# Splitting the weight chunks of two projections: casting and accumulating DMAs in place of a cast and a subtraction

## The chip, the cores and the metric

The kernel runs on one core of a Trainium2 chip. The metric is the device time of one execution in microseconds (us); lower is better.

## What is computed

One layer of an encoder on 512 tokens of width 1024: an input projection, differential attention (8 heads) beside a bidirectional state-space scan (16 heads), an output projection, a layer norm, a gated feed-forward part and a second layer norm. The two projections that the change touches are these, cut from the reference:

```python
mix = jnp.einsum('bse,ed->bsd', jnp.concatenate([attn_out, ssd_out], axis=-1), w_out[l])
x = layernorm(DEEPNORM_ALPHA * x + mix, ln1_g[l], ln1_b[l])
hid = jax.nn.silu(jnp.einsum('bsd,df->bsf', x, w_gate[l])) * jnp.einsum('bsd,df->bsf', x, w_up[l])
ffn = jnp.einsum('bsf,fd->bsd', hid, w_down[l])
x = layernorm(DEEPNORM_ALPHA * x + ffn, ln2_g[l], ln2_b[l])
```

## The kernel before

**Split operands.** TensorE multiplies in `fp32r`, a rounded 32-bit format. To keep float32 accuracy, each operand is split into a high part (rounded) and a low part (the rest), and each product is made of three matmuls: high by high, low by high, high by low (`mm3`, lines 174 to 179; in the out- and down-projections line 177 reads `wh`, line 178 reads `wl`, line 179 `wh` again).

**Weight chunks.** All weights lie in DRAM as `wall`, an array of 130 chunks of 128 x 1024 float32 (512 KB each), in the order in which they are used. Chunks 48 to 63 belong to the output projection (`I_OUT` = 48), 64 to 107 to the feed-forward part, 108 to 129 to the down-projection (`I_DN` = 108). `wload` brings a chunk into a `raw` tile by a DMA on SP's queue (`wr`); `wprep` rounds it to `wh` on ScalarE (line 106) and subtracts to get `wl` on VectorE (line 107). `raw`, `wh` and `wl` are rings of three buffers. `wget` prepares a chunk and the two after it (`AHEAD` = 2), so chunk i+2 is prepared when chunk i is asked for, into the buffers of chunk i-1.

**Out- and down-projection.** `outer_units` runs over chunks: each chunk holds two blocks of 128 rows, each block is multiplied for four tiles of 128 tokens, 24 matmuls of 512 columns for a chunk. The output has two halves of 512 columns, each with its own pass over all rows. The first pass of the output projection (chunks 48 to 55) is woven with the last attention head and goes on behind it. The second passes (`tile_major`) run the first chunks in the same way, and prepare the last four chunks meanwhile into buffers of their own (`hold`: `holdh`, `holdl` in the output projection, `keeph`, `keepl` in the down-projection); these four are then multiplied tile by tile, so that each tile's layer norm can begin early. The down-projection splits its other operand too: `hid_split` rounds a block of `hid` on ScalarE (`hidh`) and subtracts on VectorE (`hidl`).

**Order.** Each engine runs its instructions in order, and waits at the head of its queue. The order on each queue comes from the framework's scheduler, which places the instructions by its own estimate. GpSimd's queue holds few instructions in these stages: a power for each attention head (`f`), two DMAs for each layer norm's scale and shift (`ln`, line 713), and four powers in each layer norm (`rs`, line 729). SP's queue also loads the residual input (`xr` from `in_xs`, line 716) when the attention is done.

Of the kernel before, what the change touches and what calls it, by code (L numbers as in the profile page):

```python
# [8 lines left out]
F32 = mybir.dt.float32  # L9
R32 = mybir.dt.float32r  # L10
AF = mybir.ActivationFunctionType
ALU = mybir.AluOpType
# [16 lines left out]
I_OUT = N_IN  # L29
I_FF = I_OUT + 16  # L30
I_DN = I_FF + 2 * FT
N_W = I_DN + FT
# [18 lines left out]
def encoder(ctx, tc, xt, xs, wall, wdt, consts, masks, vecs, pvec, lnv, out):  # L51
    nc = tc.nc
    V, A, G, T = nc.vector, nc.scalar, nc.gpsimd, nc.tensor
# [38 lines left out]

    wcache = {}
    AHEAD = 2

    def wload(i):
        raw = wp.tile([P, 1024], F32, tag="raw", name=f"wr{i}")
        nc.sync.dma_start(raw, wall[i])
        return raw

    def wprep(i, raw=None, h=None, l=None):
        raw = wload(i) if raw is None else raw
        if h is None:
            h = wp.tile([P, 1024], R32, tag="wh", name=f"wh{i}")
            l = wp.tile([P, 1024], R32, tag="wl", name=f"wl{i}")
        A.copy(h, raw)  # L106
        V.tensor_tensor(l, raw, h.bitcast(F32), op=ALU.subtract)  # L107
        wcache[i] = (h, l)

    def wget(i, ahead=None):  # L110
        for j in range(i, min(N_W, i + 1 + (AHEAD if ahead is None else ahead))):
            if j not in wcache:
                wprep(j)
        return wcache[i]
# [9 lines left out]
    with tc.tile_pool(name="xraw", bufs=1) as xr:  # L124
# [24 lines left out]
        for k in range(KT):  # L149
            A.copy(xh[:, k], raws[k])  # L150
            (G if k in (3, 6) else V).tensor_tensor(xl[:, k], raws[k], xh[:, k].bitcast(F32), op=ALU.subtract)
            if k == 1:
                wprep(0, wraw[0])
        wprep(1, wraw[1])
        for k in range(KT):
            T.matmul(dps[0:32], wdp[:, k], xh[:, k], start=False, stop=False)
# [808 lines left out]
    raw = wload(I_FF + 3)  # L965
# [184 lines left out]
```

## Time and profile before

| what | us |
|---|---|
| median of three runs | 866.48 (865.82 to 866.75) |
| the profiled execution | 866.58 |
| its span, first to last instruction | 864.5 |
| TensorE busy | 848.4 |
| VectorE busy | 615.4 |
| ScalarE busy | 458.4 |
| GpSimd busy | 124.3 |

The profile is that of one execution. A table of busy times tells which engine is full; the waits tell which one holds up the others; and the rows further down are read by stretch, since the stages of this kernel have different limits. Matmuls overlap, so the time of one (some 390 ns) is longer than the distance from one to the next.

### The profile page before, as it was taken

The numbers are of one execution on the slowest core, as the hardware profiler recorded it, in microseconds if no ns is written. First come the engines' busy times: TensorE is split into PE (matmuls) and PEld (weight loads), VectorE is DVE, ScalarE is ACT, GpSimd is POOL, SyncE is SP. The second block draws the span as 40 slices with busy tenths as digits, with TensorE's granted clock in tenths as the row PEclk, the third lists the DMA queues.
The fourth block names the chain that finished last, engine by engine and source line by source line (L and its number), as shares of the span: only waits on it lengthen the run. The fifth ranks groups of instructions, "written<-read, shape, count | busy, mean of one in ns | idle before, by whom it ended". The sixth has DMA issues, their size and how long they took to land.

```text
span 864.5 us, 13803 instructions
## 1 busy us (share of the span) xinstructions
PE 848.4 (98%) x5404; PEld 754.4 (87%) x5404; DVE 615.4 (71%) x1071; ACT 458.4 (53%) x895; POOL 124.3 (14%) x141
## 2 busy tenths in 40 slices
PE   7999999999999999999999999999999999999996
PEld 4798989899889898898888889999999999888885
DVE  4978778775677765777634489898888887734617
ACT  4787666767565655666622215555555565522500
POOL 4016153354500000000000023000000000000002
PEclk9999999999999999999999999999999999999998
DMA  7221211202211202111144501333332333222402
GB/s 261 93 98 49 97 51 50 97 26 74 81 45 71 73 25 88 60 60 62 51 171 146 194 1 41 132 98 104 132 107 98 118 113 137 98 104 91 147 1 97
DMA packets 23008, 78.74 MB, mean 91 GB/s; under 512 B 2688, under 2 KB 2944, under 8 KB 22944
## 3 DMA queue, kind: packets, MB, share of 16 engines
q1 hardware_dynamic: 22320, 75.60, 25.1%
q0 software_dynamic: 624, 2.27, 0.9%
q8 instruction: 42, 0.69, 0.3%
q14 instruction: 22, 0.18, 0.1%
HBM read 75.77 MB, written 2.10 MB: 90 GB/s over the span
## 4 chain that ended last, share of the span: by engine, by line
PE 68%; DVE 2%; ACT 1%; issue 1%; POOLq 0%; POOL 0%; DVEq 0%; ACTq 0%
PE M L892 13%; PE N L892 6%; PE dn L178 4%; PE dn L177 4%; PE dn L179 4%; PE wo L177 3%; PE wo L179 3%; PE wo L178 3%; PE C L892 3%; PE o L623 3%; PE s L596 2%; PE s L597 2%; PE at L611 1%; PE k L177 1%; PE k L179 1%; PE k L178 1%
## 5 line engine op out<-in xcount | busy, mean ns | idle before, releaser
L107 DVE TENSOR_TENSOR wl<-wr,wh 128x1024 fp32r<-128x1024 f32 x101 | 125.3, 1241 | 65.0 <-ACT wh L106 64.9
L106 ACT CAST wh<-wr 128x1024 fp32r<-128x1024 f32 x101 | 105.6, 1048 | 71.0 <-PE wo L179 26.5
L603 ACT ACTIVATE ss<-ss,mn 128x512 f32<-128x512 f32 x64 | 45.9, 718 | 19.7 <-DVE mn L600 19.1
L178 PE MATMUL dn<-wl,hidh 128*128 128x512 f32 x130 | 51.0, 392 | 0.0
L177 PE MATMUL dn<-wh,hidh 128*128 128x512 f32 x130 | 50.9, 392 | 0.0
L179 PE MATMUL dn<-wh,hidl 128*128 128x512 f32 x130 | 50.6, 389 | 0.0
L600 DVE CUSTOM_DVE_ANT_0 ss<-s,tab 128x512 f32<-128x512 f32 x64 | 42.7, 683 | 6.4 <-PE s L597 6.2
L898 ACT COPY e<-M 128x256 f32<-128x256 f32 x60 | 22.3, 372 | 42.1 <-PE M L892 42.0
L458 ACT ACTIVATE rE<-vals,msk 64x128 fp32r<-64x128 f32 x128 | 43.0, 392 | 2.7 <-DVE vals L341 2.1
L177 PE MATMUL wo<-wh,mixh 128*128 128x512 f32 x96 | 38.1, 397 | 0.0
L179 PE MATMUL wo<-wh,mixl 128*128 128x512 f32 x96 | 37.5, 390 | 0.0
L178 PE MATMUL wo<-wl,mixh 128*128 128x512 f32 x96 | 37.4, 390 | 0.0
L177 PE MATMUL z<-wh,xh 128*128 128x256 f32 x128 | 36.4, 286 | 1.0 <-ACT wh L106 1.0
L177 PE MATMUL v<-wh,xh 128*128 128x256 f32 x128 | 36.9, 288 | 0.0
L179 PE MATMUL v<-wh,xl 128*128 128x256 f32 x128 | 36.6, 286 | 0.0
L178 PE MATMUL v<-wl,xh 128*128 128x256 f32 x128 | 36.3, 283 | 0.0
L179 PE MATMUL z<-wh,xl 128*128 128x256 f32 x128 | 36.2, 283 | 0.0
L178 PE MATMUL z<-wl,xh 128*128 128x256 f32 x128 | 36.2, 283 | 0.0
L729 POOL TENSOR_TENSOR rs<-rs,mhalf 128x1 f32<-128x1 f32 x8 | 12.2, 1525 | 158.6 <-DVE rs L728 158.6
L713 POOL DMA_DIRECT2D ln<-in_lnv x4 | 2.3, 578 | 227.1 <-PE dn L178 208.9
L623 PE MATMUL o<-va,as 128*128 128x128 f32 x256 | 34.1, 275 | 0.1
L623 PEld LDWEIGHTS o<-va,as 128*128 128x128 f32 x256 | 31.6, 192 | 0.9 <-ACT osq L626 0.3
(358 smaller groups left out, 2938.2 us busy)
## 6 DMA issues: line engine op xcount, KB each, us to landing
wr<-in_wall SPq DMA_DIRECT2D x130, 512.0 KB, 3.5
xraw<-in_xt SPq DMA_DIRECT2D x8, 256.0 KB, 6.7
xr<-in_xs SPq DMA_DIRECT2D x4, 512.0 KB, 5.2
ln<-in_lnv POOLq DMA_DIRECT2D x4, 512.0 KB, 4.5
out_y<-xr SPq DMA_DIRECT2D x8, 256.0 KB, 2.0
msk<-in_masks SPq DMA_DIRECT2D x1, 490.0 KB, 5.7
cst<-in_consts SPq DMA_DIRECT2D x1, 448.0 KB, 6.7
vec<-in_vecs POOLq DMA_DIRECT2D x1, 168.0 KB, 6.0
```

The source lines that it names most:

```text
L106: A.copy(h, raw)
L107: V.tensor_tensor(l, raw, h.bitcast(F32), op=ALU.subtract)
L177: T.matmul(o, ah, bh, start=first and i == 0, stop=False)
L178: T.matmul(o, ah, bl, start=False, stop=False)
L179: T.matmul(o, al, bh, start=False, stop=last and i == n - 1)
L458: A.activation(r[d][e, h], vals[e, sls[t]], AF.Copy, scale=hmask[e, 4 * g + h:4 * g + h + 1])
L596: T.matmul(sbs[c], QS[:, c, sl], KS[:, c], start=True, stop=False)
L600: V.tensor_tensor_reduce(out=s, in0=sb, in1=tab[:, 384 - 128 * t:896 - 128 * t], scale=1.0, scalar=3.0e38, op0=ALU.add, op1=ALU.min, accum ...
L603: A.activation(s, s, AF.Exp, scale=-1.0, bias=mn[:, t, c:c + 1], accum_out=Z[:, t, c:c + 1])
L623: T.matmul(o, ats[t][:, kt * P:(kt + 1) * P], vv[:, kt, j * P:(j + 1) * P], start=kt == 0, stop=kt == NT - 1)
L892: T.matmul(o, x[:, k], y[:, k], start=first and n == 0, stop=last and n == 11, skip_group_check=True)
L898: mats[j]["i" + name] = A.copy(e, src)
```

## The change

For 34 chunks (50 to 63 and 110 to 129) `wprep` no longer loads a raw tile. The high part is written by a DMA from GpSimd's queue whose destination is `fp32r`, so that the values are rounded on the way. ScalarE then writes the negated high part into the low tile, and a second DMA from GpSimd's queue adds the weights from DRAM to it. The first two chunks of each projection are split as before.

```diff
+    CASTS = [*range(I_OUT + 2, I_FF), *range(I_DN + 2, N_W)]
...
     def wprep(i, raw=None, h=None, l=None):
-        raw = wload(i) if raw is None else raw
+        cast = i in CASTS
+        raw = wload(i) if raw is None and not cast else raw
         if h is None:
             h = wp.tile([P, 1024], R32, tag="wh", name=f"wh{i}")
             l = wp.tile([P, 1024], R32, tag="wl", name=f"wl{i}")
-        A.copy(h, raw)
-        V.tensor_tensor(l, raw, h.bitcast(F32), op=ALU.subtract)
+        if cast:
+
+            nc.gpsimd.dma_start(h, wall[i])
+            A.activation(l, h.bitcast(F32), AF.Copy, scale=-1.0)
+            nc.gpsimd.dma_start(l, wall[i], accum_op=ALU.add)
+        else:
+            A.copy(h, raw)
+            V.tensor_tensor(l, raw, h.bitcast(F32), op=ALU.subtract)
         wcache[i] = (h, l)
```

The change moves instructions on the queues. In the excerpts `wh53`, `wl53` and so on are the high and low tile of chunk 53; the number behind the underscore is a running number of the buffer, and line numbers of the changed kernel from 113 on are 8 higher. GpSimd's queue in the output projection, before, from the powers of heads 6 and 7 to the first layer norm:

```order
L633 TENSOR_TENSOR f6_4374<-f6_4374,mhalf_70 128x4
L633 TENSOR_TENSOR f7_4623<-f7_4623,mhalf_70 128x4
L713 DMA ln0_4812<-in_lnv 128x1024
L713 DMA ln1_4814<-in_lnv 128x1024
L729 TENSOR_TENSOR rs_4755<-rs_4755,mhalf_70 128x1 x4
```

The same queue with the change, from chunk 53 on (line 110 is the casting DMA, line 112 the accumulating one):

```order
L110 DMA wh53_4596<-in_wall 128x1024
L112 DMA wl53_4597<-in_wall 128x1024
L641 TENSOR_TENSOR f7_4619<-f7_4619,mhalf_70 128x4
L110 DMA wh54_4639<-in_wall 128x1024
L112 DMA wl54_4640<-in_wall 128x1024
L110 DMA wh55_4668<-in_wall 128x1024
L112 DMA wl55_4669<-in_wall 128x1024
L110 DMA wh56_4697<-in_wall 128x1024
L110 DMA wh57_4756<-in_wall 128x1024
L112 DMA wl56_4698<-in_wall 128x1024
L721 DMA ln0_4804<-in_lnv 128x1024
L112 DMA wl57_4757<-in_wall 128x1024
```

Up to chunk 55 each chunk's two DMAs stand one behind the other, so the next casting DMA is behind an accumulating one that waits for ScalarE. Behind these rows, with the second pass of the output projection, the four held chunks come in:

```order
L721 DMA ln1_4806<-in_lnv 128x1024
L110 DMA holdh0_4808<-in_wall 128x1024
L110 DMA wh58_4813<-in_wall 128x1024
L110 DMA holdh1_4842<-in_wall 128x1024
L112 DMA holdl0_4809<-in_wall 128x1024
L112 DMA wl58_4814<-in_wall 128x1024
L112 DMA holdl1_4843<-in_wall 128x1024
L110 DMA wh59_4847<-in_wall 128x1024
L110 DMA holdh2_4876<-in_wall 128x1024
L110 DMA holdh3_4905<-in_wall 128x1024
L112 DMA wl59_4848<-in_wall 128x1024
L112 DMA holdl2_4877<-in_wall 128x1024
```

Here the DMAs stand in batches of three of a kind. In the down-projection the queue held, before, the two `ln` loads and the norm's powers:

```order
L820 TENSOR_TENSOR T4_1_5245<-x1h_4757,T2_1_5243 128x512
L820 TENSOR_TENSOR T4_1_5245<-T4_1_5245,x1l_4758 128x512
L713 DMA ln2_8034<-in_lnv 128x1024
L713 DMA ln3_8036<-in_lnv 128x1024
L729 TENSOR_TENSOR rs_4755<-rs_4755,mhalf_70 128x1 x4
```

With the change all four `keeph` and `keepl` pairs and `ln2`, `ln3` stand among the DMAs of chunks 111 to 117, in the first pass. From chunk 119 on a pattern of three chunks repeats:

```order
L112 DMA wl118_8249<-in_wall 128x1024
L110 DMA wh119_8285<-in_wall 128x1024
L110 DMA wh120_8322<-in_wall 128x1024
L112 DMA wl119_8286<-in_wall 128x1024
L112 DMA wl120_8323<-in_wall 128x1024
L110 DMA wh121_8374<-in_wall 128x1024
L112 DMA wl121_8375<-in_wall 128x1024
L110 DMA wh122_8421<-in_wall 128x1024
L110 DMA wh123_8464<-in_wall 128x1024
L112 DMA wl122_8422<-in_wall 128x1024
L112 DMA wl123_8465<-in_wall 128x1024
L110 DMA wh124_8510<-in_wall 128x1024
```

Two chunks go in pairs (wh, wh, wl, wl) and the third alone (wh, wl). On ScalarE's queue a negation stands about where the cast of the chunk stood, on VectorE's queue the subtraction is gone.

## Rows read from the trace of the kernel before

**Rows 1.** The page, busy us, share of the span and instructions of each engine.
```profile
PE 848.4 (98%) x5404; PEld 754.4 (87%) x5404; DVE 615.4 (71%) x1071; ACT 458.4 (53%) x895; POOL 124.3 (14%) x141
```

**Rows 2.** Busy time of each engine by stretch; out-projection, then down-projection.
```profile
core 0: us, PE busy (x) PEld busy (x) DVE busy (x) ACT busy (x) POOL busy (x), PEclk, DMA share, GB/s
...
447.04:463.40 16.36, 16.36 (x74) 13.50 (x73) 3.95 (x4) 3.17 (x3) 0.00 (x0) 1.00 0.52 195
463.40:500.00 36.60, 36.60 (x164) 30.12 (x163) 20.71 (x29) 10.77 (x11) 2.30 (x3) 1.00 0.50 173
739.00:795.00 56.00, 56.00 (x250) 46.03 (x250) 26.90 (x35) 21.57 (x31) 1.12 (x2) 1.00 0.31 109
795.00:840.00 45.00, 45.00 (x239) 38.70 (x238) 19.54 (x27) 13.11 (x16) 0.00 (x0) 1.00 0.22 76
```

**Rows 3.** Waits of TensorE over the whole span, three of eight.
```profile
engine line waited for: us in total, times, longest us
PE dps L148 <- POOL warm L146: 2.5, 1, 2.5
...
PE ff L178 <- DVE x1l L752: 1.1, 1, 1.1
...
PE s L596 <- DVE mixl L389: 0.3, 1, 0.3
```

**Rows 4.** ScalarE in order of time: start, length, instruction, idle before and releaser.
```profile
430.44 1.06 ACT L106 CAST wh<-wr 128x1024 fp32r<-128x1024 f32 x1 [3.16 <-PE wo L179]
...
439.51 1.04 ACT L106 CAST wh<-wr 128x1024 fp32r<-128x1024 f32 x1 [2.38 <-PE wo L179]
...
444.54 0.28 ACT L626 ACTIVATE osq<-o 128x128 f32<-128x128 f32 x1 [3.27 <-PE o L623]
...
447.24 1.05 ACT L106 CAST wh<-wr 128x1024 fp32r<-128x1024 f32 x1 [2.33 <-PE wo L179]
452.68 1.05 ACT L106 CAST wh<-wr 128x1024 fp32r<-128x1024 f32 x1 [4.38 <-PE wo L179]
458.12 1.05 ACT L106 CAST wh<-wr 128x1024 fp32r<-128x1024 f32 x1 [4.38 <-PE wo L179]
463.56 1.05 ACT L106 CAST wh<-wr 128x1024 fp32r<-128x1024 f32 x1 [4.39 <-PE wo L179]
```

**Rows 5.** The page's costliest groups: count, busy us, mean ns, idle before.
```profile
L107 DVE TENSOR_TENSOR wl<-wr,wh 128x1024 fp32r<-128x1024 f32 x101 | 125.3, 1241 | 65.0 <-ACT wh L106 64.9
L106 ACT CAST wh<-wr 128x1024 fp32r<-128x1024 f32 x101 | 105.6, 1048 | 71.0 <-PE wo L179 26.5
```

**Rows 6.** GpSimd's `ln` loads at 741.84: issue, landing (first, then both), VectorE beside.
```profile
741.84 1.12 POOL L713 DMA_DIRECT2D ln<-in_lnv  x2 [208.89 <-PE dn L178]
...
DMA to landing us min/median/max: 4.1/4.1/4.1
...
DMA to landing us min/median/max: 4.1/4.5/4.8
...
742.02 1.30 DVE L1021 TENSOR_TENSOR hidl<-hid,hidh 128x512 fp32r<-128x512 f32 x2 [1.29 <-ACT hidh L1020]
```

**Rows 7.** SP's four `xr` loads at 444.52: issue, and issue to landing.
```profile
444.52 1.75 SPq L716 DMA_DIRECT2D xr<-in_xs  x4
...
DMA to landing us min/median/max: 3.4/5.2/6.9
```

**Rows 8.** Busy time by stretch at the end of the program, columns as in group 2.
```profile
850.00:855.00 5.00, 5.00 (x41) 4.79 (x40) 4.31 (x10) 0.00 (x0) 1.52 (x1) 1.00 0.28 105
855.00:860.00 5.00, 1.71 (x16) 1.51 (x14) 4.37 (x9) 0.00 (x0) 1.52 (x1) 0.96 0.28 105
860.00:864.00 4.00, 0.00 (x0) 0.00 (x0) 1.15 (x2) 0.00 (x0) 0.00 (x0) 0.50 0.35 131
```

## The prediction

> **What bounds the kernel now.** I read the page's busy line first: TensorE is busy 98% of the span, VectorE 71%, ScalarE 53%, GpSimd 14% [rows 1]. Such a share is a mean over stages, so the next view is the busy table by stretch [rows 2]: in the out-projection (447.04 to 500) and the down-projection (739 to 840) TensorE is busy without a gap at the full granted clock, while VectorE works 3.95 of 16.36 us, 26.90 of 56 us and 19.54 of 45 us. The list of TensorE's waits over the whole program has eight entries; those after its start that are nearest to the change are 0.3 us on `mixl` in the last attention head and 1.1 us on `x1l` behind the out-projection [rows 3]. None is a wait of an out- or down-projection matmul. So in both stages the matmuls are the bound, and whatever shortens the preparation of weights there is worth at most these 0.3 us. The profiled execution took 866.58 us, its span 864.5 us and 2.1 us around it; the median of the runs is 866.48 us, 0.1 us less. I make the sum on 866.6 us.
>
> **The beat.** A chunk is 24 matmuls. Three chunks stand in the stretch 447.04 to 463.40 [rows 2], 5.45 us each, and ScalarE's casts, each released by the end of a chunk, come at 452.68, 458.12 and 463.56 [rows 4]. The ring of `wh` has three buffers: chunk i+2 gets the buffer of chunk i-1. So from the release of the buffer to the first use there are two chunks, 10.9 us. Before, the raw chunk is in SBUF by then, and a cast of 1048 ns and a subtraction of 1241 ns are all that stands between [rows 5].
>
> **What is removed.** 34 of 101 subtractions on VectorE, 34 x 1.24 = 42 us of busy time, all beside TensorE's unbroken work: worth nothing. 34 loads on SP's queue: nothing waits on that queue there. ScalarE keeps 34 passes of the same size; I take 1.05 us plus 0.1 us of handing on, 1.15 us.
>
> **What is added** for each of 34 chunks, one after another: a casting DMA, the negation, an accumulating DMA. Two of these three come out of GpSimd's queue, which is in order: an accumulating DMA that waits for ScalarE holds the next chunk's casting DMA behind it.
>
> *A plain DMA from that queue.* The trace has four of the same 512 KB, the `ln` loads [rows 6]. The one at 741.84 lands 4.1 us after its issue; its neighbour, issued some 0.58 us later, needs 4.8 us, so it lands 1.3 us after the first. The four `xr` loads go out within 1.75 us and land 3.4 to 6.9 us after issue [rows 7]: first at 447.9, last at about 452.7, 1.6 us apart. So DMAs of 512 KB in flight together follow each other. I take 2.8 us of fixed time and 1.3 us of transfer; a casting DMA moves the same bytes, so 4.1 us alone.
>
> *An accumulating DMA* is not in the trace. Write 2.8 us + x. Lower bound: x = 1.3, the bytes of a plain one. Upper bound: x = 3.9, three transfers (weights read, tile read, tile written, one after the other). I take x = 2.6: the DMA engines must read the 512 KB of weights and also the 512 KB that ScalarE left in the tile. Below the lower bound there is nothing, since no plain DMA of this queue lands faster. The Trainium skill, "Collectives: The Full Stack", section "The bandwidth ceiling", says that an adding DMA is slower for its two source reads and not for the add, and gives a ratio of 1.93; by it x would be about 2.5 us and the sum about 31 us. No run here shows it yet.
>
> *One cycle of the queue in alternating order* (wl, next wh, next wl, as in the out-projection's excerpt): wl is issued at 0 and lands at 2.8 + x; the next wh goes behind it and lands 1.3 us later; 1.15 us on ScalarE; then the next wl. That is 5.25 + x = 7.85 us against a chunk of 5.45 us: 2.4 us late for each chunk, as soon as the cover of 10.9 us is used up.
>
> **The sum, by stretches.**
> (a) Chunks 53 to 56. wh53 can go at 439.5 (the cast that chunk 50 released stands at 439.51 [rows 4]), so wl53 goes at 439.5 + 4.1 + 1.15 = 444.75, into the four `xr` loads of 444.52 [rows 7]. After the first of these has landed at 447.9, three of them, wl53 and wh54 are still to transfer: 3.9 + 2.6 + 1.3 = 7.8 us, so wh54 lands at 455.7, ScalarE is through at 456.85, wl54 lands 5.4 us later at 462.25. TensorE would start chunk 54 at 457.9: 4.35 us late. Chunks 55 and 56 lose 2.4 us each. Together 9.2 us.
> (b) Chunks 57 to 59, where the four held chunks are prepared too. Between wl56 and wl59 the queue has 8 plain transfers (ln0, ln1, wh58, wh59, four holdh) and 5 accumulating ones (wl57 to wl59, two holdl): 10.4 + 13 = 23.4 us, against three chunks, 16.35 us: 7.05 us. The order is in batches of three: after the first of three has landed, 1.15 + 2.8 us pass until an accumulating transfer can follow, of which 2.6 us are filled by the two others: 1.35 us idle for each of two batches, 2.7 us. Together 9.75 us.
> (c) Chunks 111 to 118: 14 plain (8 wh, four keeph, ln2, ln3) and 12 accumulating: 18.2 + 31.2 = 49.4 us against 8 x 5.45 = 43.6 us: 5.8 us, and 2.7 us for two batches: 8.5 us.
> (d) Chunks 119 to 125: 2.4 us at 119, then twice the pattern of three chunks in the last excerpt, whose second leg has two accumulating transfers: (5.25 + x) + (5.25 + 2x) = 10.5 + 3x = 18.3 us against 16.35 us, 1.95 us each: 6.3 us in all.
> Sum 9.2 + 9.75 + 8.5 + 6.3 = 33.8 us. Head 7 and chunks 50 to 52 I cost at nothing: there a chunk takes 7 to 9 us, since attention work stands between (casts at 430.44, 439.51, 447.24 [rows 4]), and the softmax work behind a late negation on ScalarE has gaps of 2 to 3 us ahead of it. Without that cover each 1 us by which a negation is late would reach the exponentials. The last four chunks are held ready, and the closing norms find GpSimd's queue empty: nothing. So **866.6 + 33.8 = 900 us**.
>
> **Rivals.**
> *The add costs no more than a plain DMA* (x = 1.3): (a) 3.95, (b) 3.25, (c) 33.8 us against 43.6, nothing, (d) 1.1 and 14.4 against 16.35, so 1.1. Sum 8.3 us, 875 us. For it: the same bytes come from HBM. Against it: the tile must be read as well. From x = 1.95 on the pattern of three costs time.
> *The add or the cast costs a transfer more* (x = 3.9): (a) 14.35, (b) 16.25, (c) 24.1, (d) 15.4, sum 70 us, 937 us; a casting DMA of 2.6 us besides would go to about 960. The granted clock belongs here: it stays at 1.00 up to 855 us, has a mean of 0.96 in the 5 us in which the last 16 matmuls end, and then 0.50, the level of 1.2 GHz, with TensorE idle [rows 8], so a stop of TensorE of several us, as in (b), could be followed by matmuls at the lower level.
> *VectorE holds the queue up.* Each issue of 0.58 us would wait for the VectorE instruction that runs, 0.69 to 1.23 us; 1.2 us more in a cycle is like x = 3.8, near 934 us. Against it: the two `ln` issues of 741.84 to 742.96 ran while VectorE did a `TENSOR_TENSOR` from 742.02 on [rows 6], and landed at 4.1 and 4.8 us. The Trainium skill, "SBUF — State Buffer", section "SBUF: two separate sides", says that a DMA from GpSimd cannot get its descriptors written while VectorE runs an instruction in a two-port mode; by that rule it is the copies that hold it up, and the trace shows nothing of it for a subtraction.
> *Not slower:* the transfers overlap instead of following each other, and each DMA lands 4.1 us after its issue whatever else is in flight. Then 4.1 + 1.15 + 4.1 = 9.35 us fit under the cover of 10.9 us, the queue's cycle is 0.58 + 4.1 + 1.15 = 5.83 us, and the 0.4 us by which it exceeds a chunk is eaten in (a) by the 1.55 us to spare. 866.6 to 867.5 us. It decides from the point where an accumulating DMA with a neighbour lands within 5.6 us. Against it: the neighbours of [rows 6] and [rows 7].
>
> **How the numbers follow.** The forecast, x between about 2 and 3.3, 885 to 918 us: 0.52. The cheap add: 0.18. The dear add, or VectorE in the way: 0.25, of it 0.1 beyond 960 us. Not slower: 0.05. The range goes from 872 to 960 us; it leaves out the last case and the far end of the dear one. A measurement of this kernel can tell about 0.2%, 1.7 us. Slower 0.95, same 0.04, faster 0.01 (the most to win is 0.3 us).
>
> **What would show it.** Right: waits of TensorE at the line of `wl` (the second matmul of mm3) on a DMA, 30 us or so in all, the most in 57 to 59 and 111 to 114; landings of accumulating DMAs near 5.4 us alone and 7 to 9 us in the batches; GpSimd's queue waiting for ScalarE's negations. Wrong: waits on `wh` instead, no waits at all, a landing of the accumulating DMA near 4.1 us or above 7 us when alone, or an issue on GpSimd much longer than 0.58 us.

## The result and the profile after

The changed kernel takes 922.97 us, median of four runs (922.41 to 923.56), against 866.62 us (865.82 to 867.17) for the kernel before on the same chip: ratio 1.0649, 95% interval 1.0637 to 1.0662. It is 56 us slower. The forecast was 900 us with a range of 872 to 960 us; the direction was right, the size was not: 33.5 us were forecast and 56.4 us were lost. The time lies in the range, but not in its main case (885 to 918 us); it lies where the prediction had a dearer add or VectorE in the way, and neither of these is what happened. The span of the profiled execution went from 864.5 to 920.4 us.

The changed kernel: the page's busy time of the engines, which answers [rows 1], then the DMA issues of GpSimd's queue (KB each, median us from issue to landing).

```profile
PE 865.7 (94%) x5404; PEld 762.3 (83%) x5404; DVE 575.8 (63%) x1037; ACT 458.8 (50%) x895; POOL 172.2 (19%) x209
...
wh<-in_wall POOLq DMA_DIRECT2D x26, 512.0 KB, 6.1
wl<-in_wall POOLq DMA_DIRECT2D x26, 512.0 KB, 5.4
...
holdh<-in_wall POOLq DMA_DIRECT2D x4, 512.0 KB, 11.1
holdl<-in_wall POOLq DMA_DIRECT2D x4, 512.0 KB, 8.3
keeph<-in_wall POOLq DMA_DIRECT2D x4, 512.0 KB, 6.9
keepl<-in_wall POOLq DMA_DIRECT2D x4, 512.0 KB, 9.5
```

VectorE has 39.6 us less to do, as the diff says, and it is worth nothing. TensorE was the bound; now its waits have two new lines ahead of all others, which answer [rows 3]. Waits of TensorE in the changed kernel (us in total, times, longest):

```profile
PE dn L186 <- DMA wl<-in_wall: 18.2, 7, 4.7
PE wo L186 <- DMA wl<-in_wall: 18.1, 7, 5.5
```

Line 186 is the second matmul of `mm3`, the first that reads `wl`: 36.3 us in 14 waits, all of them on accumulating DMAs and none on `wh`. One by one (start, length, instruction, wait before it and its releaser):

```profile
455.24 0.50 PE L186 MATMUL wo<-wl,mixh 128*128 128x512 f32 x1 [2.12 <-DMA wl<-in_wall]
...
464.28 0.69 PE L186 MATMUL wo<-wl,mixh 128*128 128x512 f32 x1 [3.31 <-DMA wl<-in_wall]
...
472.70 0.50 PE L186 MATMUL wo<-wl,mixh 128*128 128x512 f32 x1 [0.62 <-DMA wl<-in_wall]
...
481.03 0.50 PE L186 MATMUL wo<-wl,mixh 128*128 128x512 f32 x1 [1.55 <-DMA wl<-in_wall]
...
487.18 0.50 PE L186 MATMUL wo<-wl,mixh 128*128 128x512 f32 x1 [0.38 <-DMA wl<-in_wall]
...
499.05 0.80 PE L186 MATMUL wo<-wl,mixh 128*128 128x512 f32 x1 [5.46 <-DMA wl<-in_wall]
...
510.85 0.80 PE L186 MATMUL wo<-wl,mixh 128*128 128x512 f32 x1 [4.72 <-DMA wl<-in_wall]
...
784.58 0.80 PE L186 MATMUL dn<-wl,hidh 128*128 128x512 f32 x1 [4.68 <-DMA wl<-in_wall]
...
798.33 0.50 PE L186 MATMUL dn<-wl,hidh 128*128 128x512 f32 x1 [1.32 <-DMA wl<-in_wall]
...
807.27 0.50 PE L186 MATMUL dn<-wl,hidh 128*128 128x512 f32 x1 [2.71 <-DMA wl<-in_wall]
...
821.73 0.50 PE L186 MATMUL dn<-wl,hidh 128*128 128x512 f32 x1 [3.65 <-DMA wl<-in_wall]
...
842.45 0.50 PE L186 MATMUL dn<-wl,hidh 128*128 128x512 f32 x1 [2.12 <-DMA wl<-in_wall]
...
863.25 0.50 PE L186 MATMUL dn<-wl,hidh 128*128 128x512 f32 x1 [2.28 <-DMA wl<-in_wall]
...
883.12 0.50 PE L186 MATMUL dn<-wl,hidh 128*128 128x512 f32 x1 [1.43 <-DMA wl<-in_wall]
```

They belong to chunks 53 to 59, then 111, 113, 114, 116, 119, 122 and 125. A wait is not yet a loss: a late chunk can also run slower afterwards, and that puts off the waits behind it. TensorE is busy 17.3 us longer (848.4 to 865.7 us) for the same 5404 matmuls, and the waits and this longer work together make up the loss ahead of the last matmul (36.3 + 17.3 = 53.6 us). The loss is read by laying the two traces side by side: the first `wl` matmul of chunk 53 starts at 452.70 before and at 455.24 after, so TensorE is 2.54 us behind there. How much it falls behind in each stretch of the forecast, in the one execution that was traced (us):

| stretch, chunks | forecast | lost | of it waits on `wl` |
|---|---|---|---|
| (a) 53 to 56 | 9.2 | 11.4 | 7.6 |
| (b) 57 to 59 | 9.75 | 15.0 | 10.6 |
| (c) 111 to 118 | 8.5 | 17.3 | 12.4 |
| (d) 119 to 125 | 6.3 | 9.8 | 5.8 |
| behind the last matmul | 0 | 2.0 | |
| sum | 33.8 | 55.5 | 36.3 |

Between the stretches, in head 7 and from the last chunk on, TensorE falls behind by at most 0.3 us.

How one chunk comes about is seen on GpSimd's queue, chunks 54 and 55, and on ScalarE:

```profile
458.82 0.88 POOL L112 DMA_DIRECT2D wl<-in_wall  x1 [10.46 <-ACT wl L111]
459.37 0.88 POOL L110 DMA_DIRECT2D wh<-in_wall  x1
467.41 0.87 POOL L112 DMA_DIRECT2D wl<-in_wall  x1 [7.15 <-ACT wl L111]
467.96 0.87 POOL L110 DMA_DIRECT2D wh<-in_wall  x1
...
466.05 1.06 ACT L111 ACTIVATE wl<-wh 128x1024 fp32r<-128x1024 f32 x1 [7.54 <-DMA wh<-in_wall]
```

wl54 is issued at 458.82 and lands after 5.4 us. wh55 is issued right behind it, at 459.37, lands after 6.6 us, at 465.98, and ScalarE, which has waited 7.54 us for it, negates from 466.05 to 467.11; at 467.41 wl55 goes out, and wh56 behind that. The queue itself waited 7.15 us for ScalarE. From wl54 to wl55 it is 8.59 us, and a chunk of matmuls is 5.45 us.

### The profile page after: what moved, and what is told of

It reads as the page before. It is cut to its first block, busy times and chain, and to the rows that moved or that the text cites. A ratio compares the mean times of both kernels' runs of the same rounds, so it can differ in the third digit from the quotient of the medians.

```text
span 920.4 us, 13811 instructions
## 1 busy us (share of the span) xinstructions
PE 865.7 (94%) x5404; PEld 762.3 (83%) x5404; DVE 575.8 (63%) x1037; ACT 458.8 (50%) x895; POOL 172.2 (19%) x209
## 4 chain that ended last, share of the span: by engine, by line
PE 29%; issue 12%; DMA 4%; POOL 4%; DVE 1%; ACT 1%; POOLq 0%; DVEq 0%; ACTq 0%
PE M L900 12%; PE N L900 6%; DMA wh<-in_wall 3%; PE C L900 3%; POOL wl L112 1%; DMA wl<-in_wall 1%; PE wo L186 1%; PE wo L187 1%; POOL wh L110 1%; PE dn L186 1%; PE dn L187 1%; PE wo L185 1%; PE dn L185 1%; ACT wl L111 1%; PE ff L186 1%
## 5 line engine op out<-in xcount | busy, mean ns | idle before, releaser
L115 DVE TENSOR_TENSOR wl<-wr,wh 128x1024 fp32r<-128x1024 f32 x75 | 93.3, 1244 | 52.5 <-ACT wh L114 52.5
L114 ACT CAST wh<-wr 128x1024 fp32r<-128x1024 f32 x75 | 78.5, 1048 | 26.5 <-issue 12.9
L111 ACT ACTIVATE wl<-wh 128x1024 fp32r<-128x1024 f32 x26 | 27.5, 1059 | 88.7 <-DMA wh<-in_wall 74.4
L110 POOL DMA_DIRECT2D wh<-in_wall x26 | 17.9, 688 | 240.0 <-PE C L900 193.4
L186 PE MATMUL wo<-wl,mixh 128*128 128x512 f32 x96 | 41.0, 427 | 18.1 <-DMA wl<-in_wall 18.1
L186 PEld LDWEIGHTS dn<-wl,hidh 128*128 128x128 f32 x130 | 26.0, 200 | 26.0 <-DMA wl<-in_wall 20.9
L730 DVE SCALAR_TENSOR_TENSOR xr<-xr,dn 128x512 f32<-128x512 f32 x7 | 4.7, 685 | 66.4 <-PE dn L187 66.3
L1029 DVE TENSOR_TENSOR hidl<-hid,hidh 128x512 fp32r<-128x512 f32 x32 | 20.7, 687 | 38.0 <-ACT hidh L1028 38.0
L112 POOL DMA_DIRECT2D wl<-in_wall x26 | 22.6, 869 | 113.3 <-ACT wl L111 103.9
L186 PEld LDWEIGHTS wo<-wl,mixh 128*128 128x128 f32 x96 | 19.6, 204 | 24.9 <-DMA wl<-in_wall 21.0
```

Source lines behind the costliest of these rows:

```text
L110: nc.gpsimd.dma_start(h, wall[i])
L111: A.activation(l, h.bitcast(F32), AF.Copy, scale=-1.0)
L112: nc.gpsimd.dma_start(l, wall[i], accum_op=ALU.add)
L186: T.matmul(o, ah, bl, start=False, stop=False)
```

## The experiments

The theory after this reading: GpSimd's queue works off a series, landing of `wh`, negation, accumulating DMA, next `wh`, and each casting DMA stands behind an accumulating one that it has nothing to do with; where the held chunks come in, the transfers are too many besides. The rivals: the casting DMA is slow as such (descriptors, VectorE); the accumulating DMA is slow wherever it stands; the latency of one chunk is too long for its cover; the lower granted clock costs on top. What each run lost by stretch, read as above (us; the 2 us behind the last matmul are not in it). Each row is one execution, and executions of one variant differ by up to 5.7 us in all, so small differences between rows say nothing:

| run | (a) | (b) | held chunks 60 to 63 | (c) | (d) | median us |
|---|---|---|---|---|---|---|
| the change | 11.4 | 15.0 | 0 | 17.3 | 9.8 | 922.97 |
| casting DMA alone | 0.4 | 2.5 | 0 | 0 | 1.0 | 870.03 |
| accumulating DMA alone | 0.6 | 16.5 | 0 | 0.4 | 7.7 | 890.79 |
| second DMA without adding | 4.8 | 6.6 | 0 | 4.9 | 2.5 | 888.47 |
| without held chunks | 11.7 | 7.3 | 0 | 14.7 | 9.1 | 911.87 |
| four buffers | 6.2 | 0 | 11.2 | 7.9 | 9.0 | 901.76 |
| four buffers, hoisted | 0 | 4.0 | 6.2 | 7.5 | 0.2 | 885.61 |
| the same without held chunks | 1.5 | 4.8 | 0 | 0 | 3.9 | 878.48 |
| out-projection alone | 10.1 | 14.6 | 0 | 0 | 0 | 892.31 |
| every second chunk | 3.9 | 12.0 | 0 | 11.3 | 1.7 | 893.79 |
| the same without held chunks | 3.9 | 6.4 | 0 | 1.3 | 4.2 | 882.32 |

### The casting DMA alone

```diff
-            A.activation(l, h.bitcast(F32), AF.Copy, scale=-1.0)
-            nc.gpsimd.dma_start(l, wall[i], accum_op=ALU.add)
+            V.tensor_tensor(l, raw, h.bitcast(F32), op=ALU.subtract)
```

(and `raw` loaded for every chunk.)

> The casting DMA alone: the high part comes by GpSimd's queue as in the change, the low part is again raw load (SP's queue) and VectorE's subtraction. Theory (the serial order landing, negation, accumulating DMA, next casting DMA on one queue costs the time): no DMA of GpSimd's queue waits for ScalarE any more, a casting DMA lands 3.8 to 3.9 us after its buffer is free and the subtraction takes 1.24 us, 5.2 us under a cover of 10.9 us: 866 to 869 us, no waits of TensorE in either stage. Rival (weights by GpSimd's queue are slow as such, from the issue or from VectorE beside it): at least a third of the 56 us stays, above 885 us.

Measured: 870.03 us, ratio 1.0037 (1.0024 to 1.0051), 1 us above the theory's range. 34 casting DMAs by GpSimd's queue cost 3.3 us, and no wait of TensorE in the two projections is on one of them: at chunk 122 it waits 0.7 us for `hidl`, and the one long wait is at chunk 59, on a subtraction that stands behind those of two held chunks on VectorE (waits of TensorE):

```profile
PE wo L185 <- DVE wl L111: 2.2, 1, 2.2
```

The rival that weights by this queue are slow as such, or that VectorE's subtractions hold its issues up, is out.

### The accumulating DMA alone

```diff
-            nc.gpsimd.dma_start(h, wall[i])
+            A.copy(h, raw)
```

> The accumulating DMA alone: raw load on SP's queue and cast on ScalarE as before, then negation and accumulating DMA as in the change. Theory: one DMA per chunk on GpSimd's queue, none behind a DMA that it feeds; from the buffer's release 1.05 us cast, 1.06 us negation, 0.3 us, 5.3 us landing, 7.7 us under 10.9 us, and a queue cycle below a chunk: 866 to 871 us (the last for the held chunks). Rival (the accumulating DMA itself is the cost, wherever it stands): more than half of the 56 us stays, above 895 us.

Measured: 890.79 us, ratio 1.0274 (1.0259 to 1.0289), between the two. Away from the held chunks it is as the theory has it: (a) 0.6 us and (c) 0.4 us, with the same accumulating DMAs. But (b) loses 16.5 us, more than with the whole change: four held chunks and three others, each with a raw load and an accumulating DMA, want to go in three chunks' time. The stretch by busy time of each engine, granted clock, DMA share and GB/s:

```profile
477.57:500.43 22.86, 13.25 (x48) 10.19 (x48) 2.45 (x2) 8.09 (x8) 2.57 (x3) 0.82 1.01 274
```

The 16 DMA engines are busy all the time (1.01) while TensorE has work for 13.25 of 22.86 us. Six accumulating DMAs land in it, and six raw loads; the bytes agree, since 274 GB/s over 22.86 us are 6.26 MB, twelve transfers of 512 KB. With 1.3 us for each raw load an accumulating transfer comes to (22.86 - 7.8) / 6 = 2.5 us (estimate). The 7.7 us in (d) go where this run prepares the held chunks of the down-projection (their accumulating DMAs are issued from 822.6 to 844.8).

### The second DMA without adding

```diff
-            nc.gpsimd.dma_start(l, wall[i], accum_op=ALU.add)
+            nc.gpsimd.dma_start(l, wall[i])
```

> The second DMA of each chunk loads the weights without adding: same queue, same waits, same order. This leaves out the adding, so the low part is wrong by the high part. Theory (transfer of the accumulating DMA is 2.5 us against 1.3 us, and the queue's cycle 8.6 us against a chunk of 5.45): the cycle becomes 7.3 us; waits go from 36 us to 12 to 18 us, the lower granted clock from 12 us to 0 to 5 us, so 880 to 893 us. Rival (the add makes the whole cost): 866 to 870 us. Rival (the order makes it, whatever the transfer): 915 to 923 us.

Measured: 888.47 us, ratio 1.0249 (1.0218 to 1.0280); waits on `wl` 12.3 us. As the theory has it: wl55 now lands 3.8 us after its issue instead of 5.3, and the issues of wl54 and wl55 are 6.5 us apart instead of 8.59. 34 us of the 56 hang on the adding; 22 us stay with a plain second DMA in the same order.

### TensorE kept busy in its waits

```diff
+    FILL = {54: 11, 58: 20, 59: 17, 111: 17, 116: 13, 119: 7, 122: 7}
...
+                        for _ in range(FILL[i0 + c]):
+                            T.matmul(b, zero, h[:, i, o:o + w], start=False, stop=False)
```

> The changed kernel with 92 more matmuls with a zero tile as the stationary operand, 7 to 20 of them ahead of the second matmul of chunks 54, 58, 59, 111, 116, 119 and 122, where TensorE waited longest and the granted clock fell afterwards. They add zeros: 20.9 us more work for TensorE, placed into waits. Theory A (the matmuls at the lower level, 12.4 us by the stretches' busy time and granted clock, come on top of the waits): the clock stays at 1.00 and the time falls to 909 to 913 us. Theory B (GpSimd's queue is the bound and the slow matmuls only fill what would be waits): the clock stays up, the waits take its place, 920 to 924 us. By the releasers both hold in part (in the down-projection casting DMAs wait for TensorE, behind the held chunks they don't): 913 to 919 us is my guess.

Measured: 932.73 us, ratio 1.0752 (1.0730 to 1.0774), slower than either theory. From chunk 57 on it is no clean run: GpSimd's queue has another order there (wh57 stands behind wl56 instead of ahead of it). Up to there it is, and it answers the question. Chunks 54 and 55, first in the changed kernel, then in the filled one:

```profile
464.28 0.69 PE L186 MATMUL wo<-wl,mixh 128*128 128x512 f32 x1 [3.31 <-DMA wl<-in_wall]
472.70 0.50 PE L186 MATMUL wo<-wl,mixh 128*128 128x512 f32 x1 [0.62 <-DMA wl<-in_wall]
```

```profile
464.27 0.50 PE L682 MATMUL wo<-wl,mixh 128*128 128x512 f32 x1 [1.13 <-DMA wl<-in_wall]
...
472.68 0.62 PE L189 MATMUL wo<-wl,mixh 128*128 128x512 f32 x1 [2.23 <-DMA wl<-in_wall]
```

With fillers chunk 54 was not slowed, and the next wait was longer by the same 1.6 us. The start at 472.7 did not move: wl55 sets it.

The same with fillers only at 58, 59 and 122, which leaves the queue's order as it is:

```diff
+    FILL = {58: 20, 59: 17, 122: 7}
```

> The filled kernel of the earlier run with fillers at chunks 58, 59 and 122 alone (20, 17 and 7 matmuls with a zero tile), with which the order on GpSimd's queue is the changed kernel's own. In the changed kernel these three chunks ran 1.3, 2.4 and 1.7 us longer at the lower granted clock. Theory A (this comes on top of the waits): 5.3 us less, 917 to 918.5 us. Theory B (a slow chunk only fills the next wait): 922 to 924 us. By place: 58 is followed by a wait on a DMA that was issued without waiting for TensorE, so nothing; 59 is followed by held chunks that are ready, so 1.7 to 2.4 us; 122 is followed by a casting DMA that waits for TensorE, so 0 to 1.7 us: 919 to 921.5 us.

Measured: 926.70 us, ratio 1.0687 (1.0671 to 1.0703). Chunk 58, first in the changed kernel, then in this one (busy time by engine, granted clock, DMA share, GB/s):

```profile
499.05:505.00 5.95, 5.95 (x20) 4.84 (x21) 0.00 (x0) 0.92 (x1) 0.00 (x0) 0.76 1.08 348
```

```profile
498.80:504.50 5.70, 5.70 (x25) 4.73 (x26) 0.00 (x0) 0.61 (x1) 0.00 (x0) 1.00 1.08 361
```

The clock stayed at 1.00 instead of 0.76 (a mean of its two levels), and the first `wl` matmul of chunk 59 started at 510.55 instead of 510.85 us: once more TensorE was fast and waited longer. Theory B holds at chunk 58. At chunk 59 the fillers did not keep the clock up (it is 0.50 from 512 to 515 us in this run), so what a full clock would have won there is not shown. In the down-projection it can't be read: this run lost 21.8 us in (c), 4.5 us more than the changed kernel, ahead of the only filler there, and I found no cause for it.

### Without the held chunks

```diff
-    CASTS = [*range(I_OUT + 2, I_FF), *range(I_DN + 2, N_W)]
+    CASTS = [*range(I_OUT + 2, I_FF - 4), *range(I_DN + 2, N_W - 4)]
```

> The change without the eight held chunks (60 to 63, 126 to 129), which are prepared as before; 26 chunks stay. Theory (two causes: the serial order costs about 3 us for each plain chunk at a queue cycle of 8.5 us, and where held chunks come in as well, the transfers themselves, 1.3 us plain and 2.6 us accumulating, exceed the matmuls' time): chunks 53 to 56 lose 11.5 us as before, 57 to 59 some 9 to 10 us instead of 15, 111 to 118 10 to 12 us instead of 17, 119 to 125 8 to 10 us: 905 to 911 us. Rival (the held chunks are what costs; the plain ones are late only because of them): below 890 us.

Measured: 911.87 us, ratio 1.0515 (1.0500 to 1.0531). That is 0.9 us above the theory's range. (a) and (d) come near the theory's numbers, (b) loses less than the 9 to 10 us expected; (c) loses 14.7 us, more than the 10 to 12 expected, though its transfers (ten plain, eight accumulating) take 16 us less than with held chunks. So most of what (c) loses is not the held chunks' transfers.

### Four buffers, and the order changed

Every fourth chunk takes its two tiles from the idle raw ring, and a chunk is begun three chunks ahead:

```diff
+            q = ("raw", "raw") if cast and i % 4 == 3 else ("wh", "wl")
...
+        more = AHEAD + 1 if i + 2 in CASTS else AHEAD
```

> The change with one chunk more ahead: every fourth chunk's two tiles come out of the idle raw ring, so that four chunks have buffers and a chunk is begun three chunks ahead (cover 16.3 us instead of 10.9). The order on GpSimd's queue stays alternating. Theory (the queue's cycle of 8.5 us is the bound): a longer cover only puts the first late chunk off, about one chunk's 5.5 us for each of the two stages: 909 to 916 us. Rival (the latency is the cause: 3.9 us casting DMA, 1.4 us ScalarE and 5.3 us accumulating DMA, 10.6 us, leave 0.3 us of the cover): with 16.3 us it fits, below 885 us.

Measured: 901.76 us, ratio 1.0394 (1.0377 to 1.0411), below the theory's range and far above the rival's. The cycle is still there where the order alternates, but the casting DMAs of chunks 55 and 59, whose tiles were free early, went ahead, so that two accumulating DMAs stood together now and then. And the cover made a new wait: ScalarE's negations, now further ahead, wait for their casting DMA in front of work that TensorE needs. Waits of TensorE:

```profile
PE dn L187 <- ACT hidh L1030: 6.3, 1, 6.3
PE wo L188 <- DMA holdl<-in_wall: 6.2, 3, 2.6
PE dn L188 <- DMA wl<-in_wall: 4.8, 3, 3.9
PE wo L187 <- ACT mixh L398: 4.2, 1, 4.2
```

Then the accumulating DMA of chunk i is queued behind the casting DMA of chunk i+1:

```diff
+            with tc.issue_after(last[0]):
+                nc.gpsimd.dma_start(l, wall[i], accum_op=ALU.add)
```

> The same four buffers, and the accumulating DMA of chunk i is queued behind the casting DMA of chunk i+1, so that no casting DMA stands behind an accumulating one that waits for the casting DMA's own negation. Theory (serial order): a chunk then costs its transfers, 1.3 + 2.6 = 3.9 us against 5.45 us; no loss at chunks 53 to 56 and 119 to 125, and at the held chunks what the transfers exceed the matmuls' time by, 3 to 8 us for each of the two stages: 872 to 884 us. Rival (the transfers as such are the bound, or accumulating DMAs wait for something else): not below 905 us.

Measured: 885.61 us, ratio 1.0212 (1.0197 to 1.0228), 1.6 us above the theory's range. (a) is down from 11.4 to 0 and (d) from 9.8 to 0.2 us, with all 34 accumulating DMAs in place; four buffers in the old order had left 6.2 and 9.0 us there (4.2 and 6.3 of them the waits on `mixh` and `hidh` above), so in these two stretches it is the order. In (c) the new order adds nothing to the four buffers (7.5 against 7.9 us). A stretch of it, columns as above:

```profile
449.00:474.00 25.00, 25.00 (x113) 20.67 (x113) 5.93 (x13) 4.82 (x5) 7.38 (x11) 1.00 0.99 270
```

TensorE has no gap, though the DMA engines are at 0.99. What is left lies at the held chunks. Those taken out as well:

```diff
-    CASTS = [*range(I_OUT + 2, I_FF), *range(I_DN + 2, N_W)]
+    CASTS = [*range(I_OUT + 2, I_FF - 4), *range(I_DN + 2, N_W - 4)]
```

(with the raw ring's turn at i % 4 == 0 in the out-projection and 2 in the down-projection.)

> Both causes taken away at once: four buffers with the accumulating DMA behind the next casting DMA (as in the hoisted run), and the eight held chunks prepared as before; 26 chunks stay. Theory (serial order on GpSimd's queue plus transfers of the held chunks, and nothing else): nothing is left, 866 to 870 us, no waits of TensorE on `wl` above a few tenths of a us. Rival (a third cause, such as the landing of an accumulating DMA behind SP's loads or the clock): 875 us or more.

Measured: 878.48 us, ratio 1.0128 (1.0110 to 1.0145). A miss by 8 us, and a time in the rival's range: (c) is at 0.0, down from 17.3 us, but 1.5 us go in (a), 4.8 in (b) and 3.9 in (d). The new order and the fourth buffer came together here, so the run does not tell which of them (c) needed. In (b) SP's raw loads of the held chunks come in a row while the DMA engines are at 0.95 (470 to 492 us), and wl59 lands only 8.9 us after its issue; in (d) TensorE waits 1.8 us for a `hidh` cast on ScalarE. Both are loads and an order that this variant brought in, so the rival of a third cause in the change itself is not shown, nor is it excluded.

### The out-projection alone

```diff
+    CASTS = [*range(I_OUT + 2, I_FF)]
```

> The change in the out-projection alone (14 chunks). Theory (the stages are independent): the out-projection loses its 26.7 us, the rest nothing, and the 2 us behind the last store are gone, as in the runs with 34 DMAs on GpSimd's queue: 893 us (892 to 895). Rival (the stages share something, or those 2 us belong to any accumulating DMA): 889 or less, or 895 to 897 us.

Measured: 892.31 us, ratio 1.0294 (1.0277 to 1.0311). 24.7 us go in the out-projection's stretches, nothing in the down-projection or behind the last matmul: the out-projection's loss does not need the other stage's change.

### Every second chunk

```diff
+    CASTS = [*range(I_OUT + 2, I_FF, 2), *range(I_DN + 2, N_W, 2)]
```

> The change for chunks 50, 52, ... alone (17 of 34). Theory: a queue cycle of 8.5 us against two chunks, 10.9 us: no loss at plain chunks, 2 to 4 us at the held chunks of the out-projection, less at those of the down-projection: 867 to 874 us. Rival (latency: 3.9 us casting DMA, 1.4 us ScalarE, 5.3 us accumulating DMA come to 10.6 us against a cover of 10.9 us, so that any neighbour on the DMA engines makes a chunk late): 1 to 2 us for most of the 13 plain ones, 880 to 892 us.

Measured: 893.79 us, ratio 1.0308 (1.0292 to 1.0324). A clear miss of the time: half the chunks, and still 27 us. By place it is not the rival either, since plain chunks lose little (1.7 us in (d)). One wait is 10.1 us long, at chunk 58. GpSimd's queue ahead of it:

```profile
480.50 0.89 POOL L112 DMA_DIRECT2D holdl<-in_wall  x1 [6.31 <-ACT holdl L111]
481.91 0.89 POOL L112 DMA_DIRECT2D holdl<-in_wall  x1 [0.52 <-ACT holdl L111]
483.23 0.86 POOL L112 DMA_DIRECT2D wl<-in_wall  x1 [0.43 <-ACT wl L111]
```

wl58 stands behind the accumulating DMAs of two held chunks that are needed two chunks later than it or more, and lands 11.3 us after its issue. The last run takes the held ones away:

```diff
+    CASTS = [*range(I_OUT + 2, I_FF - 4, 2), *range(I_DN + 2, N_W - 4, 2)]
```

> Every second chunk as in the run before, and the held chunks prepared as in the kernel before: 13 of 34 chunks are left, none of them beside held ones. In the run with every second chunk 12 us went at chunk 58 and 11 us at 112 and 114, where accumulating DMAs of held chunks stood ahead of the chunk's own, 3.9 us at 54, beside the four `xr` loads, and 2 us from 116 on. Theory (the held chunks on the same queue cost the 23 us; a plain chunk with two chunks' time costs nothing but what a neighbour's loads put on it): 871 to 877 us, nothing above 1 us at 58. Rival (the loss at 58, 112 and 114 is the chunk's own latency of 10.6 us under a cover of 10.9 us): 885 us or more.

Measured: 882.32 us, ratio 1.0194 (1.0172 to 1.0216), between the theories. 12 us of the 27 are gone, (c) falls from 11.3 to 1.3 us, and four plain chunks (56, 114, 116, 118) lose 0.2 us or less, 112 and 120 some 0.9 and 0.6. But 54, 58 and 122 still lose 3.9, 6.4 and 3.5 us, each beside other loads: the four `xr` loads at 54, and SP's raw loads at 58 and 122; wl58 needs 8.2 us to land instead of 5.3. So the latency rival is right in part. One chunk alone takes 3.8 + 1.4 + 5.4 = 10.6 us of a cover of 10.9 us, and 0.3 us is no room for any neighbour.

## Why the prediction was right, and where it fell short

- **What bounds the kernel, and that VectorE's work is worth nothing**: right. 39.6 us less on VectorE, and no gain at any place.
- **A plain DMA from this queue, 4.1 us**: right. A casting DMA lands 3.8 to 3.9 us after its issue when alone, and 1.2 to 1.3 us behind another in a row.
- **The accumulating DMA, 5.4 us alone (x = 2.6)**: right for one alone, 5.2 to 5.5 us. The dear add was the rival with x = 3.9, and no landing of one alone shows that (it would be 6.7 us). In a row it costs no more: 2.5 us (estimate) in the run with the accumulating DMA alone, and in the changed kernel wl58 landed 2.55 us behind an accumulating DMA (496.46 and 499.01). The Trainium skill, "Collectives: The Full Stack", section "The bandwidth ceiling: the fold count and why AG ≠ RS ≠ AR", gives a ratio of 1.93 between the rates of an all-gather and a reduce-scatter, which is a step between ranks and not a DMA like this one; here the ratio is 2.0 (2.55 us behind another one, against 1.3 us for plain ones).
- **The queue's cycle, 7.85 us**: the mechanism is right, the size 0.74 us short. A casting DMA landed 1.75 us behind the accumulating one instead of 1.3 us (5.4 us after 458.82 and 6.6 us after 459.37), and from its landing to the next issue it took 1.43 us (465.98 to 467.41) instead of 1.15. With two such cycles in each pattern of three chunks it is most of what (d) lost beyond the forecast, 3.5 us. Of the 2.2 us in (a) it is some 0.6.
- **Stretch (a), chunk 53**: wl53 was issued at 445.33 (forecast 444.75) into the `xr` loads, landed after 9.9 us, and was itself late by 2.1 us; the forecast had only chunk 54 late. wh54 behind it landed at 457.38 (forecast 455.7), and chunk 54 put TensorE 5.9 us behind instead of 4.35: the other 1.5 us of (a).
- **Stretch (c), 8.5 us, lost 17.3**: this step failed. It was worked out as a balance of transfers against eight chunks, with the serial order counted for two batches only. The run without held chunks has room in that balance, 13 + 8 x 2.6 = 33.8 us against 43.6, and lost 14.7 us all the same; with the order changed, a fourth buffer and the held chunks gone it lost 0.0. So a balance is not enough: the wait of each chunk's round trip had to be counted too. It is open how much of this the new order takes away and how much the fourth buffer: four buffers alone brought (c) from 17.3 to 7.9 us, but with them some casting DMAs went ahead as well, and four buffers in the old order without the held chunks were not run. Also wh111 had to wait, behind a `keeph` that waited for a buffer of the FFN (GpSimd's queue):

```profile
766.88 0.56 POOL L110 DMA_DIRECT2D keeph<-in_wall  x1 [7.67 <-PE N L900]
768.62 0.55 POOL L721 DMA_DIRECT2D ln<-in_lnv  x1 [1.19 <-PE dn L186]
769.16 0.54 POOL L110 DMA_DIRECT2D wh<-in_wall  x1
```

- **Stretch (b), 9.75 us, lost 15.0**: the batches were right in kind and too small. In the run without held chunks (b) lost 7.3 us, close to three chunks at the forecast's 2.4 us; the held chunks' share, 7.7 us, was forecast at about 2.5. From the landing of wl56 (480.98) to that of wl59 (510.81) it is 29.8 us, where the forecast has 23.4 + 2.7 = 26.1. In it ln0 and wl57 took 6.15 us (to 487.13) instead of 3.9, and why is open; a raw load of SP for the FFN that was not counted took some 1.1 us; and the idle time of the two batches came to 3.3 us instead of 2.7 (in the first the casting DMA landed at 492.18, and the accumulating one, 2.6 us long, at 496.46). With the end of chunk 59 at the lower clock, 1.7 us, that makes up the 5.3 us beyond the forecast (estimate).
- **The granted clock**: named in the dear rival as an extra cost. It does fall (0.76 at chunk 58). But fillers that kept it at 1.00 in chunks 54 and 58 moved the start of the next chunk's first `wl` matmul by 0.0 and 0.3 us: there it only fills waits. For the down-projection no run shows it. Behind chunk 59, whose successors lay ready, it is a loss: 25.0 us behind at its first `wl` matmul, 26.7 at its last. The Trainium skill, "TensorE: Matmul & The Clock Gate", section "HAM oscillation — how this bites in real kernels", says that matmuls behind a wait on a DMA run at half rate and counts that as loss; the fall is here, and at the places that could be read it is a loss only where nothing late comes next.
- **VectorE in the way of the issues**: out. The Trainium skill, "SBUF — State Buffer", section "SBUF: two separate sides", says that GpSimd cannot write a DMA's descriptors while VectorE runs an instruction in a two-port mode. Beside VectorE's subtractions no such wait shows: the issues of 26 casting DMAs took 0.54 us each in the run with the casting DMA alone (870.03 us). No run here tests a copy. In the changed kernel the issue of an accumulating DMA took 0.87 us, longer than the 0.58 us of the prediction, and without the adding 0.53 us, so that goes with the adding.
- **Not slower**: out. Its point was an accumulating DMA with a neighbour within 5.6 us; with neighbours ahead of them they took 5.8 to 12 us, and a casting DMA behind one took 6.6 us (wh55).
- **Head 7, chunks 50 to 52, the last four chunks, the norms at nothing**: right, at most 0.3 us. Not foreseen were 2.0 us behind the last matmul; they are GpSimd's `DRAIN` at the end of the program, as the last section shows.

## What to carry to other kernels

A preparation step by DMA that feeds an engine that feeds a second DMA on the same in-order queue costs the whole round trip for each item, and the next item's independent DMA pays for it; put the independent one ahead, and have a buffer more for it (both together took two stretches here from 11.4 and 9.8 us to 0 and 0.2; the order with three buffers was not run). Compare the round trip with the cover first: here 10.6 us of 10.9 left no room for any neighbour's transfer, and relieving an engine that nothing waited for paid for none of it. Where a stretch mixes urgent and non-urgent prefetches on one queue, count the order at every item, since a balance of transfers over the stretch gave half the loss here.

## What the runs showed of the hardware beyond that

The span ends later behind the last matmul, by a time that goes with the number of these DMAs on GpSimd's queue: nothing with 34 or fewer, 0.8 us with 52 (the two runs with 26 chunks), 2.0 to 2.5 us with 68. The last store is issued 4.5 us behind the end of the last matmul in the kernel before and in the changed one alike, so the time lies behind it. What grows is GpSimd's own `DRAIN` at the end of the program, an instruction that stands under the line `with tile.TileContext`. Instructions of that line (count, shortest/median/longest in ns, first and last start in us): before, with the casting DMA alone, without the held chunks, and two rows of the changed kernel.

```profile
L1146 POOLq DRAIN  x3: 40/102/2056, 858.1 to 864.2; - x3
...
L1153 POOLq DRAIN  x3: 46/93/4831, 861.9 to 868.0; - x3
...
L1154 POOLq DRAIN  x3: 46/93/6299, 901.0 to 907.8; - x3
...
L1154 POOLq DRAIN  x3: 46/93/7604, 912.0 to 920.1; - x3
L1154 SPq DRAIN  x3: 7/7/7, 917.6 to 919.9; - x3
```

GpSimd issued 5, 39, 57 and 73 DMAs in all in these four, and its longest `DRAIN` took 2.06, 4.83, 6.30 and 7.60 us: some 0.08 us more for each DMA (estimate). In the changed kernel it starts at 912.0 and ends at 919.6, 2 us after SP's (917.6), and the last instructions wait for it. With 34 added DMAs it ends before SP's starts (866.7 against 867.4 us with the casting DMA alone), and nothing waits for it.
